# Key rotation permuted by VectorE's writes, norm squares in bf16 with twice the places, mask loads moved past the first gates, scheduler rules and estimates revised

## The chip, the cores and the metric

One Trainium2 chip, all 8 cores running one program, one batch element each. The metric is the device time of the slowest core, in microseconds (us). A program on all cores has a second, slower state in some of its executions, in which the cores of one die have a lower granted TensorE clock; only executions of the fast state are compared here. Because the slowest of eight cores is a noisy pick, I also give the mean of the eight cores.

## The reference, cut to what matters

Two decoder layers on x of 8 x 4096 x 1024. Each layer is a SwiGLU block, a mixer and a second SwiGLU block, each behind an RMS norm with shift, scale and gate from a conditioning vector.

```python
y = modulate(rmsnorm(h, norm_g[l, 1]), sh2, sc2)
proj = y @ w_in[l]                                # u, v of the gating unit; q, k, v of the attention
out_a = spatial_gating(u_a, v_a, ...)             # v is normalised, multiplied by a causal 128 x 128 matrix, gated by u
q_b = apply_rope(q_b, cos, sin); k_b = apply_rope(k_b, cos, sin)
out_b = dilated_mixture(q_b, k_b, v_b)            # windows (128,1), (512,4), (2048,16): keys gathered by stride
h = h + g2 * (concat(out_a, out_b) @ w_out[l])
```

## The kernel before

The kernel is written as operations with an engine (or a choice of engines) and an **estimate in nanoseconds**. A list scheduler in the kernel plays these estimates through when the program is built, and so fixes the order of instructions on every engine and, where there is a choice, the engine. Each engine then runs its list strictly in order.

The rotation of q and k: four products on VectorE, two sums on GpSimd. Keys leave GpSimd permuted, so that the strided attention reads them in order. The value normalisation may go to ScalarE or GpSimd:

```python
for (x, z) in ((0, 0), (1, 1), (0, 1), (1, 0)):
    G.op([dve(lambda e, ...: e.tensor_tensor(out=ap, in0=bank(bks[x]), in1=cs[:, z, :], op=ALU.mult), 610)], ..., name="rope")
for h_ in range(2):
    fr = [[128, 4], [8, 16], [1, 8]]
    to = fr if qk == 0 else [[128, 4], [1, 16], [16, 8]]
    f = lambda e, ...: e.tensor_tensor(out=cust(o, 0, to), in0=cust(a0[0], 0, fr), in1=cust(a1[0], 0, fr), op=...)
    G.op([pool(f, 1800)], reads=[a0[1], a1[1]], writes=[bo], name="ropeadd")
    G.dma("sp", ..., 131072, reads=[bo], accw=[bd[t]], name="qkst")
# vnorm(s), for each of 4 heads
G.op([act(lambda e, ...: e.activation(out=o, in_=i_, func=AF.Identity, scale=sc, bias=bi), 390), pool(f, 500)], ..., name="vnorm")
```

The norm: ScalarE squares eight pieces of a tile into a ring of places, GpSimd adds them up, one small matmul sums over partitions, VectorE multiplies the tile by the result ("nu").

```python
sqR = Ring([NM, NM + 2048], [128, T], F32, "sq")          # also used for "nu"
```

One rule of the scheduler: an instruction whose inputs the estimate has ready later than its turn is put off only if it lies well ahead of the main chain of matmuls.

```python
if not t.dma and t.L > hp + 5000.0 and t.mready > t.ready:
    m = t.mready + min(6000.0, 0.5 * (t.L - hp - 5000.0))
```

The softmax here doesn't subtract the row's maximum and nothing guards it: scores larger than these inputs give would overflow.

Of the kernel before, what the change touches and what calls it, by code (L numbers as in the profile page):

```python
# [7 lines left out]
F32 = mybir.dt.float32  # L8
# [4 lines left out]
D = 1024  # L13
# [55 lines left out]
class Graph:  # L69
# [30 lines left out]
    def _new(self, name, pos):  # L100
        t = Task()
        t.id = len(self.tasks)
        t.name = name
        t.pos = pos
        t.cur = self.M if pos is None else pos
        t.L = None
        t.wl = None
        t.main = False
        t.due = None
        t.part = None  # L110
        t.soft = ()
        t.banks, t.new = [], []
        t.nbytes, t.dma = 0, False
        t.eng = None
        t.tok = None
        t.succ = []
        self.tasks.append(t)
        return t
# [95 lines left out]
    def schedule(self, bw=300.0, dlat=2300.0, dmargin=3000.0, cmargin=250.0, backlog=9000.0):  # L214
# [65 lines left out]
        def pick(e, now):  # L280
# [3 lines left out]
            if e == "pe":  # L284
# [4 lines left out]
                for t in av:  # L289
                    if best is not None and (t.mready <= now, -t.pos) <= bk:  # L290
                        continue
                    if t.new:
                        i, f = find_places(t.new, now)
                        if i is None:
                            nxt = min(nxt, f)
                            continue
                        n = sum(b.n for b in t.new)
                        if (t.pos > hp + 4000.0 or n > 1) and t.name != "up" and sum(x <= now for x in pfree["ps"]) < self.RESERVE + n:
                            nxt = min(nxt, max(now + 50.0, sorted(pfree["ps"])[self.RESERVE + n - 1]))
                            continue  # L300
                    best, bk = t, (t.mready <= now, -t.pos)
# [5 lines left out]
            for t in av:  # L307
# [11 lines left out]
                if not t.dma and t.L > hp + 5000.0 and t.mready > t.ready:  # L319
                    m = t.mready + min(6000.0, 0.5 * (t.L - hp - 5000.0))  # L320
                    if m > now:
# [254 lines left out]
def build_nc():  # L576
# [37 lines left out]
    with ExitStack() as st:  # L614
# [115 lines left out]
        sqR = Ring([NM, NM + 2048], [128, T], F32, "sq")  # L730
# [24 lines left out]
        def cond(chunks, pos, slots, cslot, due=None):  # L755
# [7 lines left out]
                  due=None if due is None else due - 90000.0)  # L763
# [4 lines left out]
            ring = Ring(slots, [128, D], F32, "ada")  # L768
# [33 lines left out]
        def load_gu(l, w, j, pos):  # L802
# [3 lines left out]
            if (l, w) == (0, 0) and (l, w, j) not in kept:  # L806
                G.dma("pool", lambda e: e.dma_start(out=ap, in_=wgu_d[l, w, j]), 1048576, writes=[b], name="guf", pos=pos,
                      due={0: -41000.0, 1: -31000.0, 2: -25000.0, 3: -24000.0, 4: -1000.0}.get(j), extra=[first[(8, 11, 13, 15)[min(j, 3)]]] if j < 6 else ())
# [41 lines left out]
        def main(ins, banks, name, soft=()):  # L850
            p = G.M
            t = G.chain(ins, banks, name, soft=soft)
            marks.append((p, t))
# [53 lines left out]
        def norm_y(ht, slot, l, i, pos, alts=0, apart=False):  # L907
# [6 lines left out]
            for kc in range(KC):  # L914
                hk, bh = ht.ap[:, kc, :], ht.b[kc]
                u, bu = (sq_more[0] if sq_more else sqR).take() if apart else (hk, bh)
# [28 lines left out]
        class FFN:  # L945
# [5 lines left out]
            def gates(self, tiles, slots, reset=True):  # L951
# [5 lines left out]
                for j in range(FC):  # L957
                    gu, bgu = load_gu(self.l, self.w, j, G.M)
                    for t in tiles:
                        y, by = Y[t % 4]  # L960
                        banks = [Bank(), Bank()]
                        for half in range(2):
                            bk = banks[half]
                            main([(lambda e, kc=kc, half=half, bk=bk, y=y, gu=gu: e.matmul(  # L964
                                bank(bk), lhsT=gu[:, half, kc, :], rhs=y[:, kc, :], start=(kc == 0), stop=(kc == KC - 1)),
                                [bgu, by[kc]], MM) for kc in range(KC)], [bk], "gate" if half == 0 else "up", self.act[t][1][j].last())
# [51 lines left out]
        class Mixer:  # L1018
# [24 lines left out]
            def open(self, more):  # L1043
# [3 lines left out]
                sq_more[:] = [Ring([NM, NM + 2048] + steps(more[0], 2048, 2), [128, T], F32, "sq")]  # L1047
# [40 lines left out]
            def proj(self, t):  # L1088
# [67 lines left out]
                def qkpart(qk, g):  # L1156
                    bks = [chunk(8 + qk * 4 + g * 2 + h_, False) for h_ in range(2)]
                    tt = []
                    for (x, z) in ((0, 0), (1, 1), (0, 1), (1, 0)):
                        ap, b = self.tr.take()  # L1160
                        tt.append((ap, b))
                        G.op([dve(lambda e, x=x, z=z, ap=ap: e.tensor_tensor(out=ap, in0=bank(bks[x]), in1=cs[:, z, :],  # L1162
                                                                             op=ALU.mult), 610)],
                             reads=[bks[x], bcs], writes=[b], name="rope")
                    dst, bd = (qS, bQS) if qk == 0 else (kS, bKS)
                    for h_ in range(2):
                        o, bo = self.qk.take()
                        a0, a1 = (tt[0], tt[1]) if h_ == 0 else (tt[2], tt[3])
                        fr = [[128, 4], [8, 16], [1, 8]]
                        to = fr if qk == 0 else [[128, 4], [1, 16], [16, 8]]  # L1170
                        f = lambda e, o=o, a0=a0, a1=a1, h_=h_: e.tensor_tensor(  # L1171
                            out=cust(o, 0, to), in0=cust(a0[0], 0, fr), in1=cust(a1[0], 0, fr),
                            op=ALU.add if h_ else ALU.subtract)
                        G.op([pool(f, 1800)], reads=[a0[1], a1[1]], writes=[bo], name="ropeadd")
                        to_ = bass.AP(dst.tensor, dst.offset + (g * 256 + h_ * 32) * S + t * T, [[64 * S, 4], [S, 32], [1, T]])
                        G.dma("sp", lambda e, o=o, to_=to_: e.dma_start(out=to_, in_=o), 131072, reads=[bo], accw=[bd[t]],
# [44 lines left out]
        class Attn:  # L1221
# [51 lines left out]
            def load_v(self, p, r, pos):  # L1273
# [6 lines left out]
                if r == 1:  # L1280
# [3 lines left out]
                    G.dma("sp", lambda e: e.dma_start(out=v, in_=src), 128 * (16 - n0) * 384, reads=rd, writes=[b],  # L1284
# [3 lines left out]
                for n in range(n0, SB // st_):  # L1288
                    src = bass.AP(vS.tensor, vS.offset + (T0 + n * st_) * VW + p * 192, [[r * VW, 128], [VW, r], [1, 192]])
                    i0 = (n - n0) * r  # L1290
                    G.dma("sp", lambda e, src=src, i0=i0: e.dma_start(out=v[:, i0:i0 + r, :], in_=src), 128 * r * 384,  # L1291
# [159 lines left out]
        for b_ in range(2):  # L1451
            for pc_ in range(2):
                G.dma("pool", lambda e, b_=b_, pc_=pc_: e.dma_start(
                    out=mk_sb[:, :, b_ * 256 + pc_ * 128:b_ * 256 + pc_ * 128 + 128],
                    in_=mk_d[:, :, pc_ * 256 + b_ * 128:pc_ * 256 + b_ * 128 + 128]), 196608, accw=[bC["mk"]], name="mk", pos=100000.0)
# [3 lines left out]
        for l in range(DEPTH):  # L1459
# [3 lines left out]
            def nrm(t, i, pos, src_=None, off=HB):  # L1463
                s, b = (src, bsrc) if src_ is None else src_
                first = l == 0 and i == 0
                norm_y(norm_load(t, s, b, pos, off, {0: -60000.0, 1: -26000.0}.get(t) if first else None), t % 4, l, i, pos, (1 if t == 0 else 3) if l == 0 and i == 0 and t < 4 else 0)
# [9 lines left out]
            if l == 0:  # L1476
                conv(0, 0, [(p1 + 40000.0, pg)], False)
# [207 lines left out]
```

## Time and profile before

| | kernel before |
|---|---|
| time, median of 3 runs | 4878.17 us (4877.49 to 4881.88) |
| mean of the eight cores, profiled run | 4863.5 us |
| TensorE busy, slowest core | 4758.2 of 4881.1 us |
| first gate matmul, median of the cores | 53.2 us |
| four stretches of projection, medians of the cores | 139.7 + 183.6 + 137.7 + 183.6 us |

TensorE is the bound, so a reader looks for the places where it stands still, and for what ended each wait. These groups are the ones that the rotation touches (columns: line, engine, operation, output and input, shapes, count; then busy us and mean ns; then idle time before them and what ended it), kernel before:

```profile
L1162 DVE TENSOR_TENSOR arena<-ps,arena 128x512 f32<-128x512 f32 x256 | 164.3, 681 | 63.1 <-PE ps L1102 35.9 <-POOL arena L1171 24.5 <-POOL arena L895 1.4
L1171 POOL TENSOR_TENSOR arena<-arena 128x512 bf16<-128x512 f32 x128 | 233.6, 1872 | 126.3 <-DVE arena L1162 121.7 <-DVE arena L1127 4.0 <-DVE arena L1133 0.2
L1143 POOL TENSOR_SCALAR arena<-arena 128x128 bf16<-128x128 f32 x26 | 18.9, 734 | 0.0
```

L1162 are the products, L1171 the sums (straight for q, permuted for k, mixed in one mean), L1143 the value normalisations that fell to GpSimd.

### The profile page before, as it was taken

Reading aid. Unit: us, or ns where it says so; the run is one execution under the profiler, and the core shown is the slowest. Engines: PE = TensorE matmul, PEld = TensorE weight load, DVE = VectorE, ACT = ScalarE, POOL = GpSimd, SP = SyncE. Lnnn points to the kernel's source line nnn. Section 1 sums busy time; section 2 is a strip of 40 time slices with the busy share of each in tenths; the row PEclk is TensorE's granted clock in tenths of the full one; section 3 lists DMA queues with packets and bytes.
Section 4 is the critical chain, followed back from the end, with each engine's and each line's share of the span. In section 5 each row is a group of like instructions: output and inputs, shape, how many; then the busy total and the mean of one; then the engine's idle time right before and its main releaser. Section 6 shows DMA issues by size and latency. Waiting matters only on the chain.

```text
span 4881.1 us, 74319 instructions; the slowest of 8 cores (4846.7 to 4881.1 us)
## 1 busy us (share of the span) xinstructions
PE 4758.2 (97%) x25855; PEld 2250.7 (46%) x25855; DVE 2428.5 (50%) x4088; ACT 2044.3 (42%) x3040; POOL 1053.6 (22%) x922
## 2 busy tenths in 40 slices
PE   5999999999999999999999999999999999999998
PEld 2444445444445454444444444454444455544443
DVE  5552556473655373665334326554536654535533
ACT  4111566462755352521311127655537443525311
POOL 0001551112631111310200026412136200123101
PEclk9999999999999999999999999999999999999999
DMA  8977686687575777665721375767665645473414
GB/s 233 207 165 184 171 226 163 177 233 200 160 223 145 192 219 210 208 195 141 237 84 38 92 220 148 218 153 180 154 179 175 195 135 151 117 246 129 143 42 157
DMA packets 376095, 835.31 MB, mean 171 GB/s; under 512 B 151440, under 2 KB 184592, under 8 KB 369296
## 3 DMA queue, kind: packets, MB, share of 16 engines
q1 hardware_dynamic: 356944, 742.08, 49.4%
q0 software_dynamic: 18784, 88.49, 11.7%
q8 instruction: 212, 3.47, 0.3%
q14 instruction: 155, 1.27, 0.1%
HBM read 741.72 MB, written 234.88 MB: 200 GB/s over the span
## 4 chain that ended last, share of the span: by engine, by line
PE 87%; DMA 4%; SPq 3%; ACT 2%; DVE 2%; issue 1%; POOL 1%; DVEq 0%; ACTq 0%; POOLq 0%
PE ps L964 46%; PE ps L992 24%; PE ps L1102 8%; PE ps L1426 4%; PE ps L1368 3%; PE ps L1334 2%; DMA arena<-xP 1%; DMA arena<-hS 1%; SPq L1291 1%; DMA arena<-qS 1%; DVE arena L917 1%; SPq L776 0%; SPq L1435 0%; POOL arena L895 0%; SPq L1188 0%
## 5 line engine op out<-in xcount | busy, mean ns | idle before, releaser
L964 PE MATMUL ps<-arena 128*128 128x512 bf16 x11264 | 2505.1, 380 | 44.0 <-DVE arena L921 32.4
L964 PEld LDWEIGHTS ps<-arena 128*128 128x128 bf16 x11264 | 1082.0, 98 | 1318.1 <-issue 70.4
L992 PE MATMUL ps<-arena 128*128 128x512 bf16 x5632 | 1230.5, 379 | 1.0 <-DVE arena L996 1.0
L970 ACT ACTIVATE arena<-ps 128x512 f32<-128x512 f32 x704 | 418.1, 597 | 1242.4 <-PE ps L964 1233.6
L972 DVE SCALAR_TENSOR_TENSOR arena<-arena,ps 128x512 f32<-128x512 f32 x704 | 480.7, 685 | 770.4 <-ACT arena L970 769.7
L992 PEld LDWEIGHTS ps<-arena 128*128 128x128 bf16 x5632 | 547.5, 98 | 655.7 <-issue 5.2
L895 POOL TENSOR_TENSOR arena<-arena 128x512 f32<-128x512 f32 (+1 forms) x351 | 455.8, 1299 | 1122.2 <-ACT arena L888 1029.8
L996 DVE SCALAR_TENSOR_TENSOR arena<-ps,arena 128x512 f32<-128x512 f32 x256 | 192.1, 751 | 902.4 <-PE ps L992 893.5
L977 DVE TENSOR_TENSOR arena<-ps,arena 128x512 bf16<-128x512 f32 x704 | 484.3, 690 | 202.6 <-PE ps L964 182.4
L1102 PE MATMUL ps<-arena 128*128 128x512 bf16 x2560 | 570.3, 381 | 10.0 <-ACT arena L1153 4.0
L888 ACT ACTIVATE arena<-arena 128x512 f32<-128x512 f32 x424 | 257.2, 626 | 757.2 <-DVE arena L996 387.8
L1352 ACT ACTIVATE arena<-ps 128x1024 bf16<-128x1024 f32 (+1 forms) x384 | 344.6, 949 | 294.5 <-PE ps L1334 291.9
L1102 PEld LDWEIGHTS ps<-arena 128*128 128x128 bf16 x2560 | 249.3, 98 | 309.2 <-issue 20.9
L1355 DVE TENSOR_TENSOR arena<-arena 128x1024 bf16<-128x1024 bf16 (+1 forms) x384 | 258.6, 679 | 141.1 <-ACT arena L1352 139.3
L1404 POOL TENSOR_TENSOR arena<-arena 64x512 bf16<-64x512 f32 x128 | 165.5, 1293 | 592.3 <-ACT arena L1399 545.2
L923 ACT ACTIVATE arena<-arena 128x512 bf16<-128x512 f32 x371 | 276.4, 805 | 36.8 <-DVE arena L917 36.3
L917 DVE TENSOR_TENSOR arena<-arena 128x512 f32<-128x512 f32 x384 | 261.5, 731 | 37.8 <-ACT arena L903 35.0
L1171 POOL TENSOR_TENSOR arena<-arena 128x512 bf16<-128x512 f32 x128 | 233.6, 1872 | 126.3 <-DVE arena L1162 121.7
L1426 PE MATMUL ps<-arena 128*128 128x512 bf16 x1024 | 227.1, 381 | 2.6 <-DMA arena<-mS 2.6
L1384 DVE TENSOR_TENSOR arena<-ps,arena 128x512 f32<-128x512 f32 x256 | 175.5, 685 | 69.7 <-PE ps L1368 63.6
L1368 PEld LDWEIGHTS ps<-arena 128*128 128x128 bf16 x2736 | 174.8, 98 | 76.0 <-issue 16.6
L1368 PE MATMUL ps<-arena 128*128 128x128 bf16 x2736 | 198.7, 220 | 9.1 <-DVE arena L1355 8.5
(66 smaller groups left out, 2075.2 us busy)
## 6 DMA issues: line engine op xcount, KB each, us to landing
arena<-wguS SPq DMA_DIRECT2D x242, 512.0 KB, 7.8
arena<-hS SPq DMA_DIRECT2D x180, 512.0 KB, 8.6
arena<-wdS SPq DMA_DIRECT2D x128, 704.0 KB, 6.0
arena<-ada_w SPq DMA_DIRECT2D x144, 512.0 KB, 18.0
hS<-arena SPq DMA_DIRECT2D x224, 256.0 KB, 5.2
arena<-hS SPq DMA_DIRECT2D x136, 256.0 KB, 6.8
wguS<-wgu POOLq DMA_DIRECT2D x66, 512.0 KB, 7.7
hS<-arena SPq DMA_DIRECT2D x64, 512.0 KB, 6.9
```

Source lines behind the costliest of these rows:

```text
L895: f = lambda e, a=a, sq=sq, out=out: e.tensor_tensor(out=out, in0=a, in1=sq, op=ALU.add)
L917: f = lambda e, hk=hk, u=u: e.tensor_tensor(out=u, in0=hk, in1=rs, op=ALU.mult)
L923: ga = act(lambda e, hk=hk, A=A, sh=sh, o=o: e.activation(out=o, in_=hk, func=AF.Identity, scale=A, bias=sh), 725)
L964: main([(lambda e, kc=kc, half=half, bk=bk, y=y, gu=gu: e.matmul(bank(bk), lhsT=gu[:, half, kc, :], rhs=y[:, kc, :], start=(kc == 0), stop ...
L970: G.op([act(lambda e, sg=sg, gb=gb: e.activation(out=smv[sg.i], in_=bank(gb), func=AF.Tanh, scale=0.5), 490, "tanh")], reads=[gb], writes= ...
L972: G.op([dve(lambda e, sg=sg, gb=gb: e.scalar_tensor_tensor(out=smv[sg.i], in0=smv[sg.i], scalar=1.0, in1=bank(gb), op0=ALU.add, op1=ALU.mu ...
L977: G.op([dve(lambda e, sg=sg, ub=ub, o=o: e.tensor_tensor(out=o, in0=bank(ub), in1=smv[sg.i], op=ALU.mult), 610)], reads=[ub, sg], writes=[ ...
L992: main([(lambda e, j=j: e.matmul(bank(bk), lhsT=wd[:, j, :], rhs=a[:, j, :], start=(j == 0), stop=(j == FC - 1)), [bwd, ba[j]], MM) for j ...
L1102: ins.append((lambda e, lhs=lhs, rhs=rhs, kc=kc: e.matmul(bank(bk), lhsT=lhs, rhs=rhs, start=(kc == 0), stop=(kc == KC - 1)), rd + [by[kc] ...
L1352: return e.activation(out=cut(pT, 0), in_=cut(ps[:, :, :], sb.i * 512), func=AF.Exp, scale=0.125)
L1368: return e.matmul(o, lhsT=v[:, vi, h * 64:h * 64 + 128], rhs=pT[:, h, b, pc, :], start=(pc == 0 or not prev), stop=(pc == 1))
L1426: main([(lambda e, kc=kc, m=m, bk=bk: e.matmul(bank(bk), lhsT=w[:, m, kc, :], rhs=mx[:, kc, :], start=(kc == 0), stop=(kc == KC - 1)), [bw ...
```

## The change

The intent: GpSimd's permuted writes are slow, so let VectorE write the key products permuted and GpSimd add contiguously; give the squares slack; get the mask loads out of the way of the first weights; let the scheduler be more careful. The core of it:

```diff
-sqR = Ring([NM, NM + 2048], [128, T], F32, "sq")
+sqR = Ring(steps(NM, 1024, 4), [128, T], BF16, "sq")
+nuR = Ring(steps(NM, 2048, 2), [128, T], F32, "nu")        # 8 and 4 places in the projection
...
+    def f(e, ...):
+        if qk == 0:
+            return e.tensor_tensor(out=ap, in0=bank(bks[x]), in1=cs[:, z, :], op=ALU.mult)
+        fr = [[128, 4], [8, 16], [1, 8]]
+        return e.tensor_tensor(out=cust(ap, 0, [[128, 4], [1, 16], [16, 8]]), in0=cust(bank(bks[x]), 0, fr),
+                               in1=cust(cs, z * T, fr), op=ALU.mult)
+    G.op([dve(f, 610)], ..., name="rope")                   # the estimate stays
...
-            out=cust(o, 0, to), in0=cust(a0[0], 0, fr), in1=cust(a1[0], 0, fr), ...
-        G.op([pool(f, 1800)], ..., name="ropeadd")
+            out=o, in0=a0[0], in1=a1[0], ...
+        G.op([pool(f, 1350)], ..., name="ropeadd")
...                                      # scheduler: deferral also near the main chain; "up" follows its "gate"
-    if not t.dma and t.L > hp + 5000.0 and t.mready > t.ready:
-        m = t.mready + min(6000.0, 0.5 * (t.L - hp - 5000.0))
+    if not t.dma and t.mready > t.ready:
+        m = t.mready + max(0.0, min(6000.0, 0.5 * (t.L - hp - 5000.0)))
...                                      # cost guesses of two kinds of DMA
-    G.dma("sp", ..., 131072, ..., name="qkst")
+    G.dma("sp", ..., 180000, ..., name="qkst")
-    G.dma("sp", ..., 128 * (16 - n0) * 384, ..., name="av")
+    G.dma("sp", ..., 128 * (16 - n0) * 700, ..., name="av")
...                                      # start: masks after the ninth matmul chain, weight loads gated later, x earlier
-    extra=[first[(8, 11, 13, 15)[min(j, 3)]]] if j < 6 else ()
+    extra=[first[(10, 12, 14, 15, 19)[min(j, 4)]]] if j < 6 else ()
```

## The prediction

> **What bounds the kernel now.** I read the page first, then the cores, the waits of TensorE, the chain of waits in order of time, and stretches of 20 to 200 us.
>
> The page's first part and the cores:
>
> ```profile
> PE 4758.2 (97%) x25855; PEld 2250.7 (46%) x25855; DVE 2428.5 (50%) x4088; ACT 2044.3 (42%) x3040; POOL 1053.6 (22%) x922
> core 0: 4881.1 us, clock 0.994
> core 6: 4846.7 us, clock 0.996
> ```
>
> TensorE is busy for 4758.2 of 4881.1 us: only 122.9 us of the slowest core are not matmul time. If the matmuls stay (the built orders of both kernels have 25,857 each), the time cannot fall below about 4758 us plus a start and an end, so a gain of 2% (98 us) is all but excluded. The cores run one program, yet differ by 34 us: part of what the slowest loses is late data, not arithmetic. By stretches of 200 us, core 0's idle TensorE time is 59.2 us in the first stretch, 5.0 and 8.5 in 400 to 800, 4.1 in 1000 to 1200, 7.0 and 2.9 in 1400 to 1800, 2.6 in 2000 to 2200, 3.7 and 8.7 in 2800 to 3200, about 4.6 elsewhere, and 16.6 at the end.
>
> Who ends these gaps (the waits of TensorE on core 0):
>
> ```profile
> PE ps L964 <- DVE arena L921: 32.4, 1, 32.4
> PE ps L899 <- DVE arena L895: 24.1, 2, 21.8
> PE ps L1368 <- DVE arena L1355: 8.5, 8, 4.1
> PE ps L964 <- DMA arena<-wguS: 4.9, 2, 4.5
> PE ps L899 <- POOL arena L895: 3.9, 2, 2.4
> PE ps L1102 <- ACT arena L1153: 4.0, 1, 4.0
> ```
>
> The first two are the start: nothing but one small matmul runs until the first gate at 54.7 us. The others are short stalls. The chain of waits shows what lies behind them:
>
> ```profile
> 30.96 30.44 DMA arena<-xP
> 65.48 3.57 PE ps L964 x8
> ...
> 605.49 17.47 DMA arena<-xP
> ...
> 630.88 2.36 POOL arena L1171
> ...
> 637.63 0.38 PE ps L899
> ```
>
> The start hangs on the input of tile 1, not only on the 16 modulation rows: the transfer of x lands 30 us after issue. At 605 to 638 us the chain runs from a late tile through GpSimd's key rotation (L1171) to the norm-sum matmul (L899). After a stall the matmuls are slow for a while: 8 of them take 3.57 us at 65.48, against about 0.215 us each in the undisturbed stretch 200 to 400 (929 in 200 us).
>
> **The Trainium skill.** "TensorE: Matmul & The Clock Gate", Part 1, says that the array's clock drops after an idle window of about 3.4 us and returns after a busy one. The trace agrees: 3.57 us for 8 matmuls, and 7.8 us for 24 after the 4.0 us stall at 674 us, where 24 x 0.215 = 5.2 us is normal, a second loss of 2.6 us. "DMA: Bandwidth & Descriptors", Queues, rings and completion order, says that each engine takes packets in turn from the queues that have work; so GpSimd's queue takes from SyncE's even where SyncE's transfers were issued first. The trace agrees: in 0 to 60 us the two shared the engines, which were full,
>
> ```profile
> q1 hardware_dynamic: 4115, 13.03, 72.0%
> q0 software_dynamic: 1394, 2.38, 25.1%
> ```
>
> "Advanced Engine Details and Errata", Memory Cachelines, says that an access to another 16-byte line each time costs extra in SBUF. GpSimd shows it: the 64 query rotations (contiguous) take 1.27 us, the key rotations, which write bf16 with a step of 32 bytes, about 2.4. Whether VectorE pays it too for f32 written with a step of 64 bytes no instruction of this trace shows.
>
> **The change part by part.**
>
> Key rotation. 128 products on VectorE (half of L1162's 256, 0.681 us each) now write permuted; the 64 key sums on GpSimd become contiguous. L1171 is 233.6 us for 128; 64 at 1.27 are 81, so the key half is 152.6 / 64 = 2.38 us each. Gain on GpSimd: 64 x (2.38 - 1.27) = 71 us, or 4.4 us in each of 16 tiles. The built order gives part back: GpSimd's normalisations of v go from 26 to 58, 32 x 0.73 = 23 us. On VectorE I expect 0.68 to at most 1.3 us per permuted product, so 0 to 80 us, 0 to 5 us per tile. In the projection stretches (540 to 680 us) VectorE is about 60 to 80% busy, so this hides. None of it is on TensorE; it counts only through stalls.
>
> Norm squares. Their ring goes from 2 to 4 places (8 in the projection), and scaled rows get their own. ScalarE's 0.626 us and GpSimd's 1.30 us stay (the sums stay f32). What is gained is slack: ScalarE can square ahead of GpSimd's additions. At the end of the kernel nothing moves: the built order still has both last norm-sums behind the last down matmul, so the 17 us tail stays.
>
> Start. Two of the four mask loads (in front at 1.6 us) and two more at 49 us go behind the ninth chain of matmuls; gate-weight loads 1 to 3 wait for the 13th, 15th and 16th modulation row as issued instead of the 11th, 13th and 15th, and loads 4 and 5 for tile 1's input. By windows, SyncE's queue used 39.7 us of full-engine time up to 52 us, GpSimd's 10.3 (masks 2.5, the first weight load 3.2, the rest 4.6). I expect some 5 us of the latter left, so the last row lands 5 us sooner and the first gate starts near 50 instead of 54.7 us. But the new order puts tile 1's norm sum after 16 gate matmuls, not 32. Tile 1's last squares came at 70 us, with 19.7 us of GpSimd's queue ahead; now only four weight loads are ahead, 4 x 3.2 = 12.7 us, so near 63 us. The norm sum then ends near 65 instead of 71.9 us, with 16 matmuls (3.5 us) more left to do. Net gain: 7.0 - 3.5 = 3.5 us, rather than 4.7.
>
> Scheduler. A row load for attention counts almost double (700 for 384 bytes), operations with uncertain inputs are put off more cautiously, and an up chain follows its gate. The built SyncE order changes mostly at the turns into attention: three gate-weight loads instead of one now stand between the two kinds of v loads where TensorE stalled 4.5 us on wguS at 1448 us.
>
> The sum for core 0: start -3.5. In the projection stages of both layers stalls of about 9.8 + 2.1 and 3.7 + 8.7 us, with some 12 us of slow clock behind them (clock 0.97 over two stretches of 200 us: 0.03 x 400); I estimate that 40% of these 36 us go: -14. The attention and turn stalls (4.1 + 7.0 + 2.9 + 2.6 + about 3, and 5 of clock) are about 25; a fourth goes: -6. Together -24 us: 4878 - 24 = 4854; I take 4857, since the slowest of eight cores keeps the worst stalls. The two fractions are my choice; the profile gives only the pool from which they draw.
>
> **The rivals.**
>
> A. VectorE becomes the stage's bound. If the permuted writes cost 1.3 us or more, four key products take over 5 us, about as long as the 24 matmuls beside them (5.2 us); the ring of four products and the banks then back up. For it: TensorE already waits on banks freed by VectorE and ScalarE there. Against it: two of four rotations per tile are queries, and GpSimd loses 4.4 us per tile. With 2 us lost in each of the 8 tiles least filled with other work: +16 on the sum, about 4870.
>
> B. Late inputs stay. In 655 to 673 us ScalarE waits 3.7 and 4.3 us for x before squares, and its later GELU then frees a bank late (the 4.0 us stall). More places for squares do not bring x earlier, and the new order puts norm sums 32 to 56 matmuls sooner, in trust of a faster GpSimd. If x is as late as before, TensorE stands before the norm sum: about 3 us in some four places and as much of slow clock, +24 on the sum: about 4878.
>
> C. The start is worth more, if x of tile 1 and the rows both land 7 us sooner and tile 0's four weights suffice: -7, and all stalls of projection halved: near 4840.
>
> **Range and chances.** The sum gives -24; rival A about -8, B about 0, C about -38. I widen both ends by the spread of the cores: 4830 to 4884. Faster by over 2% would need under 4780, less than matmuls plus start and tail (4758 + 50 + 17), so 1%; slower by over 2% would need 98 us of new stalls, conceivable only if VectorE's permuted writes cost several times more: 1%.
>
> **What would show it.** L1171 near 1.27 us in all 128 and the sum near 163 us; the permuted products in a row of their own, at 0.7 us (else A); the first gate near 50 us and tile 1's norm sum ending near 65; squares unchanged near 0.63 us; the waits of L1102 and L899 after 500 us lower in both layers, with the clock of 600 to 800 and 3000 to 3200 above 0.97; the tail still 17 us. I am wrong if norm sums wait longer than before (B), if ropes hold the banks (A), or if the slow cores 0, 2, 4 and 7 do not come nearer to 1, 3, 5 and 6.

## The result, and the profile after

The fast runs of the changed kernel took 4889.81, 4890.12 and 4893.37 us. Ratio to the kernel before **1.0025**, 95% interval [1.0005, 1.0045]. Ratios here are the mean time of one kernel's fast runs over that of the other's of the same rounds, so not quite the ratio of the medians. It is the class that was predicted (within 2%), but 12 us slower where 21 us faster was expected, and above the range of 4830 to 4884.

The page's first part, two of the cores, and the rotation's groups of the kernel after, in the columns shown before:

```profile
PE 4755.4 (97%) x25855; PEld 2250.5 (46%) x25855; DVE 2466.9 (50%) x4087; ACT 2026.2 (41%) x3009; POOL 987.9 (20%) x954
core 1: 4888.1 us, clock 0.995
core 3: 4860.4 us, clock 0.997
L1169 DVE TENSOR_TENSOR arena<-ps,arena 128x512 f32<-128x512 f32 x128 | 81.8, 680 | 20.6 <-PE ps L1106 14.1 <-POOL arena L1178 5.5 <-DMA arena<-rope 0.9
L1171 DVE TENSOR_TENSOR arena<-ps,arena 128x512 f32<-128x512 f32 x128 | 119.5, 1025 | 20.2 <-PE ps L1106 13.8 <-POOL arena L1178 6.1
L1178 POOL TENSOR_TENSOR arena<-arena 128x512 bf16<-128x512 f32 x128 | 168.4, 1324 | 165.8 <-DVE arena L1169 115.1 <-DVE arena L1171 45.9 <-DVE arena L1131 4.2
L1147 POOL TENSOR_SCALAR arena<-arena 128x128 bf16<-128x128 f32 x58 | 40.5, 710 | 2.6 <-DVE arena L1137 2.6
```

All busy times did what was intended: GpSimd's sums 233.6 to 168.4 us, VectorE's permuted products 1.03 us each in place of 0.68, TensorE the same. The start did too; the waits of TensorE in the first 80 us of core 0 (columns: engine, tile and line, releaser; us in total, times, longest):

```profile
PE ps L967 <- DVE arena L924: 26.9, 1, 26.9
PE ps L902 <- DVE arena L898: 19.7, 1, 19.7
PE ps L886 <- ACT arena L884: 9.8, 3, 4.7
```

The first two lines answer to the 32.4 and 21.8 us of the kernel before: the first gate comes 6 us sooner. The third is new: tile 1's squares. They end 7 us sooner than before (at 62.3 in place of 69.4 us, medians of the cores), but the order now puts them behind 16 gate matmuls instead of 32, so TensorE runs out of work before they come.

To see where the 6 us and more went, I cut the span at stages that both kernels pass (the last matmul of each group of gates, downs and projections), on every core, and compared the medians over the cores. On two of the eight cores of every profile some 2% of the matmul records are missing; there a stage ends at the gap between two groups, not at a count. (The expectations below quote an earlier cut without this care; it was up to 1 us off in the projections of these two kernels and about 3 us in layer 0's attention.) Differences to before: start -6.2; gates and downs of tiles 0 to 3 of layer 0 +2.2; **the four stretches of projection +6.2, +3.5, +4.6 and +2.5, together +16.8**; the gates and downs of tiles 4 to 7 -5.6; **the second half of the attention** (the second SwiGLU's gates and downs 0, 1 and gates 2, 3, beside which it runs) **-0.1 in layer 0 and +5.2 in layer 1**; the tail 17.7 us in both. All differences together are 11.9; the mean of the cores rose by 12.0. Layer 0's first projection took 136 to 137 us on four cores of the kernel before and 143 to 147 on the other four, so its median lies between two groups; layer 1's is the cleaner measure: 136 to 139 us on seven of the cores before, 140 to 146 on all eight after.

The waits of TensorE in layer 1's first projection, core 2, kernel before (2941 to 3078 us) and then kernel after (2939 to 3082 us):

```profile
PE ps L1102 <- ACT arena L1118: 2.1, 1, 2.1
PE ps L1193 <- ACT arena L923: 1.8, 1, 1.8
PE ps L1102 <- ACT arena L1145: 0.7, 1, 0.7
```

```profile
PE ps L1199 <- POOL arena L1147: 3.9, 3, 1.6
PE ps L1106 <- ACT arena L1122: 2.7, 1, 2.7
PE ps L1106 <- ACT arena L1149: 0.7, 1, 0.7
```

The new wait is that of the gating matmuls (L1199) for value normalisations on GpSimd (L1147). (L1118, after L1122, is the values' GELU, L1145 or L1149 the normalisation on ScalarE, L923 or L926 the scaling of the normed tile, L1157 the GELU of u.) Averaged over the cores, the waits of this stretch are 8.3 us after against 5.2 before; in layer 0's first projection 10.3 against 6.7. Why such a normalisation is late is seen on the engines' timelines of the same core (start, duration, then as above; x5 is five in a row):

```profile
2959.82 6.15 DVE L920 TENSOR_TENSOR arena<-arena 128x512 f32<-128x512 f32 x8
2961.61 5.53 POOL L1147 TENSOR_SCALAR arena<-arena 128x128 bf16<-128x128 f32 x5
2965.58 0.22 PE L1199 MATMUL ps<-arena 128*128 128x128 bf16 x1 [1.37 <-POOL arena L1147]
2967.40 0.22 PE L1199 MATMUL ps<-arena 128*128 128x128 bf16 x1 [1.60 <-POOL arena L1147]
```

Five normalisations take 5.53 us while VectorE multiplies two operands from SBUF (L920); of the 58 on a core, 14 lie beside L920 and take 0.9 to 1.9 us, and the other 44, beside key products (PSUM and one SBUF operand) or nothing, take 0.44. The Trainium skill, "SBUF — State Buffer", Who interferes with whom, states this: a VectorE instruction with two SBUF inputs contends with a GpSimd instruction that reads SBUF; their shared ports are an exclusive lock, and the order of issue decides which of the two blocks. It made a tempting theory, which the experiments below did not bear out as the cause of the loss.

### The profile page after: what moved, and what is told of

Its sections match the earlier page's. It is cut to its first block, busy times and chain, and to the rows that moved or that the text cites. A ratio compares the mean times of both kernels' runs of the same rounds, so it can differ in the third digit from the quotient of the medians.

```text
span 4888.1 us, 74266 instructions; the slowest of 8 cores (4860.4 to 4888.1 us)
## 1 busy us (share of the span) xinstructions
PE 4755.4 (97%) x25855; PEld 2250.5 (46%) x25855; DVE 2466.9 (50%) x4087; ACT 2026.2 (41%) x3009; POOL 987.9 (20%) x954
## 4 chain that ended last, share of the span: by engine, by line
PE 86%; DMA 5%; ACT 3%; DVE 2%; issue 2%; SPq 1%; POOL 1%; DVEq 0%; ACTq 0%; POOLq 0%
PE ps L967 47%; PE ps L995 24%; PE ps L1106 5%; PE ps L1432 4%; PE ps L1374 3%; PE ps L1340 2%; DMA arena<-xP 1%; DMA hS<-arena 1%; DMA arena<-hS 1%; DVE arena L1171 1%; ACT arena L1149 1%; DMA kS<-arena 0%; POOL arena L1147 0%; SPq L778 0%; POOL arena L1178 0%
## 5 line engine op out<-in xcount | busy, mean ns | idle before, releaser
L898 POOL TENSOR_TENSOR arena<-arena 128x512 f32<-128x512 f32 (+2 forms) x351 | 414.3, 1180 | 1160.4 <-ACT arena L891 1056.9
L891 ACT ACTIVATE arena<-arena 128x512 bf16<-128x512 f32 x424 | 250.5, 625 | 723.9 <-DVE arena L999 384.6
L1361 DVE TENSOR_TENSOR arena<-arena 128x1024 bf16<-128x1024 bf16 (+1 forms) x384 | 261.5, 687 | 148.7 <-ACT arena L1358 146.4
L926 ACT ACTIVATE arena<-arena 128x512 bf16<-128x512 f32 x372 | 279.5, 806 | 52.3 <-DVE arena L920 51.9
L920 DVE TENSOR_TENSOR arena<-arena 128x512 f32<-128x512 f32 x384 | 271.9, 757 | 35.7 <-ACT arena L906 30.4
L1410 POOL TENSOR_TENSOR arena<-arena 64x512 bf16<-64x512 f32 x128 | 168.4, 1316 | 598.5 <-ACT arena L1405 557.9
L1374 PEld LDWEIGHTS ps<-arena 128*128 128x128 bf16 x2736 | 175.4, 98 | 73.8 <-issue 12.9
L1374 PE MATMUL ps<-arena 128*128 128x128 bf16 x2736 | 199.2, 219 | 7.4 <-DVE arena L1361 6.8
L1178 POOL TENSOR_TENSOR arena<-arena 128x512 bf16<-128x512 f32 x128 | 168.4, 1324 | 165.8 <-DVE arena L1169 115.1
```

The lines of the kernel that those rows point to most:

```text
L898: f = lambda e, a=a, sq=sq, out=out: e.tensor_tensor(out=out, in0=a, in1=sq, op=ALU.add)
L920: f = lambda e, hk=hk, u=u: e.tensor_tensor(out=u, in0=hk, in1=rs, op=ALU.mult)
L926: ga = act(lambda e, hk=hk, A=A, sh=sh, o=o: e.activation(out=o, in_=hk, func=AF.Identity, scale=A, bias=sh), 725)
L1374: return e.matmul(o, lhsT=v[:, vi, h * 64:h * 64 + 128], rhs=pT[:, h, b, pc, :], start=(pc == 0 or not prev), stop=(pc == 1))
```

## The experiments

Theory 1: the dearer permuted writes lose. Theory 2: the order that the scheduler builds loses, through its rules, its guesses, or the estimate 1350. Theory 3: the normalisations on GpSimd lose. All results below are of fast runs (three to five in each row, from five rounds), beside the kernel before on the same chip. "Slowest" and "mean" are differences in us to the before of the same rounds (slowest core, mean of cores; means over the fast runs). "Proj." is the sum over the four projection stretches, "att." the second half of the attention in both layers, each against before, medians over the cores of the profiled run; one profile each, so differences of 2 us or less in them mean little. In one run each of x3 and x8, two of x9 and three of x1, cores of one die show a slightly lower clock (0.98 to 0.99), too little to be counted as slow; this lengthens the slowest core above all. (The mean of the changed kernel, 4877.0, is held against the 4863.5 of the profiled run of before.)

| run | edit | slowest | mean | ratio [95%] | start | proj. | att. |
|---|---|---|---|---|---|---|---|
| after | the whole change | +12.2 | +13.5 | 1.0025 [1.0005, 1.0045] | -6.2 | +16.8 | +5.0 |
| x1 | start alone | +14.6 | +0.8 | 1.0029 [0.9995, 1.0064] | -7.0 | +5.3 | -1.5 |
| x2 | rotation, estimate 1800 | -3.3 | -4.0 | 0.9992 [0.9976, 1.0008] | -0.2 | -2.8 | -2.6 |
| x3 | after, straight products | +6.5 | +7.5 | 1.0013 [0.9993, 1.0033] | -7.1 | +12.1 | +3.0 |
| x4 | after, GpSimd permutes | +19.8 | +21.3 | 1.0040 [1.0024, 1.0056] | -6.8 | +28.0 | +6.8 |
| x5 | rotation, estimate 1350 | +13.9 | +19.0 | 1.0028 [1.0014, 1.0042] | -0.5 | +11.2 | +3.3 |
| x6 | squares alone | -1.0 | +5.0 | 0.9998 [0.9985, 1.0011] | -1.1 | +1.6 | +1.1 |
| x7 | rules and guesses alone | +3.1 | +3.3 | 1.0004 [0.9985, 1.0023] | -0.6 | +5.8 | +3.1 |
| x8 | after, old rules and guesses | +25.9 | +24.2 | 1.0053 [1.0020, 1.0086] | -7.3 | +16.6 | +5.6 |
| x9 | after, estimate 1800 | +16.1 | +6.6 | 1.0034 [0.9976, 1.0091] | -7.3 | +0.1 | +3.0 |
| x10 | after, no normalisation on GpSimd | +24.4 | +30.9 | 1.0051 [1.0035, 1.0067] | -6.4 | +25.1 | +9.1 |
| x11 | x5, no normalisation on GpSimd | +26.3 | +30.4 | 1.0057 [1.0039, 1.0075] | +0.7 | +18.8 | +4.7 |
| x12 | before, estimate 1350 | +27.4 | +32.8 | 1.0057 [1.0039, 1.0075] | +0.1 | +19.3 | +5.6 |
| x13 | after, fills for normalisations | +7.9 | +9.4 | 1.0016 [1.0000, 1.0032] | -6.8 | +15.8 | +5.0 |
| x14 | after, 1800, old guesses | -2.7 | -1.9 | 0.9992 [0.9971, 1.0014] | -7.1 | +0.2 | 0.0 |
| x15 | after, key products at 1040 | **-10.5** | **-7.4** | **0.9979 [0.9963, 0.9994]** | -7.3 | -0.2 | +1.9 |
| x16 | x14, normalisations to VectorE | +10.1 | +12.1 | 1.0021 [1.0005, 1.0036] | -6.7 | +9.5 | +2.9 |
| x17 | x5, key products at 1040 | +3.1 | +4.9 | 1.0005 [0.9991, 1.0019] | +0.7 | +2.7 | +1.8 |
| x18 | x15, old guesses | -10.3 | -1.9 | 0.9979 [0.9966, 0.9991] | -6.4 | -0.7 | +1.1 |

### x1 to x4: the parts, and the writes against the order

**x1**, the start alone (masks, gates of the weight loads, x earlier; no other hunk).

> The kernel before with the start's part alone (mask loads behind the ninth chain, later gates for the first weight loads, order of the modulation rows). In the changed kernel the first gate came about 6 us earlier and 1 to 2 us were given back in the first gates stage. If the start's gain does not depend on the other parts: first gate near 47 us, 4 to 5 us faster than before in the mean of the cores, all later stages within 1 us, about 4874 us. If the start only moves work into the crowded stage that follows: 0, about 4878 us.

The first gate came 7.0 us sooner, yet the mean of the cores was the same as before; the gain went in the following stages (gates and downs of tiles 0 to 3 +3.4, projections +5.3). Its slowest core varied from 4876 to 4915 us, so the slowest core alone would mislead.

**x2**, the rotation's instructions in the exact order of before. Only the estimate keeps that order:

```diff
-        G.op([pool(f, 1350)], reads=[a0[1], a1[1]], ...)
+        G.op([pool(f, 1800)], reads=[a0[1], a1[1]], ...)
```

> The kernel before, in exactly its order of instructions, with only the key rotation changed (VectorE writes permuted, GpSimd adds contiguous). Theory 1, the permuted writes cost more than they save (1.03 instead of 0.68 us, 44 us in all, in stages where VectorE feeds the banks): the projection stages 4 to 6 us longer each in the first half and 2 to 3 in the second, about 4890 us. Theory 2, the operations are a gain and the new order loses it: 2 to 6 us faster than before, about 4874 us, key sums at 1.27 us.

The same permuted products, at the same price, in the run x2:

```profile
L1167 DVE TENSOR_TENSOR arena<-ps,arena 128x512 f32<-128x512 f32 x128 | 121.2, 1030 | 17.3 <-PE ps L1102 15.5 <-POOL arena L1174 1.7
```

The kernel was 4.0 us faster in the mean of cores, and all projections together 2.8 us shorter than before. So the rotation does not lose by what its instructions cost.

**x3**, the changed kernel's order with straight key products (wrong result, relative error 0.152), and **x4**, the same order with GpSimd permuting as before:

```diff
-                            if qk == 0:
+                            if qk < 2:            # x3; x4 in addition writes the sums of k permuted on GpSimd
```

> The changed kernel in exactly its order, but key products written straight on VectorE (keys stay unpermuted: wrong result on purpose). Theory 1: products 0.68 us, the projection stages 10 to 14 us shorter in all than in the changed kernel, about 4877 us. Theory 2: VectorE is 44 us less busy, but the stages stay within 3 us of the changed kernel, about 4888 us.

> The changed kernel in exactly its order, with the key rotation as before (straight products on VectorE, permuted sums on GpSimd at 2.4 us; correct result). Theory 1: close to the time before or below it, 4872 to 4880 us, because VectorE's 44 us go and the start's gain stays. Theory 2: the order counts on a GpSimd that is now 71 us busier: longer than the changed kernel by 5 to 15 us, 4895 to 4905 us.

In the changed order, straight products take the projections' loss from +16.8 to +12.1: about a quarter of it comes with the permuted writes, three quarters stay without them. x4's sums, the line to hold against L1178 above:

```profile
L1178 POOL TENSOR_TENSOR arena<-arena 128x512 bf16<-128x512 f32 x128 | 233.6, 1891 | 147.8 <-DVE arena L1169 145.3 <-DVE arena L1131 1.3 <-DMA qS<-arena 0.6
```

With them the projections lose 28.0 us in that order, against 16.8: moving the permutation to VectorE is right, in either order. Theory 1 falls as the main cause.

### x5 to x8: which part of the new order

**x5** is x2 with the change's estimate of 1350, so it differs from x2 by one number. **x6** is the squares alone, **x7** the scheduler's rules and DMA guesses alone, **x8** the change without those.

> Kernel before with the key rotation of the change and its new estimate for the GpSimd sums (1350 in place of 1800); nothing else. By the built order the value normalisations on GpSimd rise from 26 to 54 of 128, which is the only thing that distinguishes it from the run with the old order (4875.6 us mean, 4 us under the kernel before in the mean of cores). Theory 'estimate': the lower estimate makes GpSimd look free and the scheduler gives it normalisations in the projection stages, for whose release TensorE then waits: the first projection stage (139.7 us before, 141.9 with the old order) goes to 144 to 147, the span to about 4885. Theory 'rules': the loss of the changed order comes from the scheduler's new rules, not from this estimate: span 4873 to 4880, first projection stage at most 143. Neither expects anything in the second half of the attention (its three stages together within 1 us of before).

> Kernel before with the squares in bf16, four places and their own ring for the products, alone. Theory 'squares gain': GpSimd's sums of norms are 0.12 us cheaper each and the squares run earlier, so the stalls of the start and of the reloads fall slightly: span 4873 to 4878. Theory 'reordering': every shift of the greedy schedule deals the waits anew, with no systematic gain: span 4874 to 4888, with the squares of the next norm run ahead of the values' products and stores, so that the stage after the first projection starts with the late key load. If the second half of the attention loses 3 us a layer here, the ring of squares is its cause.

> Kernel before with only the scheduler's new rules and estimates (the deferral of instructions that would make an engine wait, the pairing of gate and up, the higher cost guesses of two kinds of DMA); no arithmetic, tile or engine form changes. Theory 'rules': these alone lose what the changed kernel loses in the second half of the attention (3 us a layer there) and part of the projection: span 4884 to 4892, the mean of cores 4869 to 4876. Theory 'rotation': the rules are neutral, span 4874 to 4882, and no stage moves by more than 2 us.

> The changed kernel with the scheduler's old rules and old DMA guesses: rotation (with the new estimate), squares and start only. Theory 'rules': it keeps the start's 6 us, loses nothing in the second half of the attention, and lands at 4870 to 4880. Theory 'estimate': the 56 normalisations on GpSimd stay, so the first projection stage stays at 144 or more and the span at 4882 to 4892.

x5 answers: the same instructions, one estimate changed, and the mean of cores goes from -4.0 to +19.0, the projections from -2.8 to +11.2. My stage figure for layer 0's first projection missed (142.0 us, expected 144 to 147), layer 1's (143.1 us, 137.7 before) shows it instead. x6 is neutral on the slowest core, though 5 us worse in the mean of cores. x7 is nearly neutral, and shows where layer 1's second half of the attention loses; I had expected 4884 to 4892 under the theory of rules, and it was 4881.5. x8 is worse than the changed kernel, also without its one run with a disturbed die (+14.6 and +21.9 then): the new rules and guesses do not cause the loss but lessen it.

### x9 to x12: the estimate, and the normalisations on GpSimd

**x9** puts 1800 back in the changed kernel; **x12** puts 1350 into the kernel before, with no other edit. **x10** and **x11** forbid GpSimd the normalisations:

```diff
-                            out=o, in_=i_, func=AF.Identity, scale=sc, bias=bi), 390), pool(f, 500)],
+                            out=o, in_=i_, func=AF.Identity, scale=sc, bias=bi), 390)],
```

> The changed kernel with one number put back: the estimate of GpSimd's sum of rotated products, 1350 to 1800. Arithmetic, tiles and engine forms are those of the changed kernel; the normalisations on GpSimd fall from 58 to 38. Theory 'estimate' (now the leading one: rotation with the old estimate was 4 us faster in the mean of cores, with the new one 19 us slower): this recovers most of the loss: slowest core 4872 to 4882 (the changed kernel: 4890), mean of cores 4858 to 4866 (changed: 4877), and the first projection stage of layer 0 at 143 us or less (changed: 146.2), of layer 1 at 140 or less (142.7). Theory 'any reordering loses': this is just one more order of the same greedy schedule and lands anywhere from 4876 to 4895, with the projection stages no better than the changed kernel's.

> The changed kernel with its estimates, but the values' normalisations allowed on ScalarE alone (0 of 128 on GpSimd in place of 58). Theory 'normalisations': it is these that the low estimate lets onto GpSimd, two tenths of a microsecond longer there and queued ahead of the sums, so this recovers as much as the old estimate: slowest core 4874 to 4882, layer 1's first projection at 140 or less. Theory 'sums early': the loss is how early the low estimate makes the scheduler place the sums and what waits behind them, the normalisations are a bystander: 4884 to 4894, the projection stages within 1.5 us of the changed kernel's. ScalarE becomes busier in the projection, so a loss above 4894 would say that GpSimd's help was needed.

> The kernel before with the key rotation of the change and its new estimate (that run was 4892 us, 4878.5 in the mean of cores), and the values' normalisations on ScalarE alone (0 in place of 54). Theory 'normalisations': back to 4874 to 4880, mean of cores 4857 to 4863. Theory 'sums early': 4885 to 4894, as with the 54.

> The kernel before, its arithmetic and engine forms untouched (GpSimd still writes the keys permuted, 2.4 us in place of 1.3), with the new estimate of 1350 alone. Theory 'estimate': the order built from that number is what loses, whoever permutes: 4888 to 4900, at least as slow as the run with the rotation and the new estimate (4892), because GpSimd's sums are longer still. Theory 'permuted writes on VectorE': with straight products the order costs nothing: 4875 to 4882.

x9's projections are back at the length of before (+0.1 in place of +16.8). Its slowest core is inconclusive: two runs took 4872.3 and 4873.7 us, two others 4901 and 4929 with one die at a clock of 0.98 to 0.99. x12 loses 19.3 us in the projections with not one instruction form changed: **the estimate alone makes a loss of this size**. (At 4905 us it is a little slower than the 4888 to 4900 expected.) x10 and x11 refute theory 3 in its plain form: with no normalisation on GpSimd the projections are worse still; ScalarE is then the one waited for.

### x13 to x16: the port, the guesses, and true numbers

**x13** keeps the changed kernel's order on every engine and replaces the normalisations on GpSimd by fills, which read nothing (wrong, relative error 0.143). **x14** is x9 with the old DMA guesses. **x15** changes one number of the changed kernel to what the trace shows. **x16** is x14 with the normalisations on ScalarE or VectorE, at an estimate of 250 for VectorE.

```diff
-    f = lambda e, ...: e.tensor_scalar(out=o, in0=i_, scalar1=sc, scalar2=bi, op0=ALU.mult, op1=ALU.add)
+    f = lambda e, o=o: e.memset(o, 0.0)                                  # x13
...
-    G.op([dve(f, 610)], reads=[bks[x], bcs], writes=[b], name="rope")
+    G.op([dve(f, 610 if qk == 0 else 1040)], reads=[bks[x], bcs], writes=[b], name="rope")      # x15
...
-    ... bias=bi), 390), pool(f, 500)],
+    ... bias=bi), 390), dve(f, 250)],                                    # x16
```

> The changed kernel in its exact order on every engine; only the 58 value normalisations that GpSimd does are replaced by a fill of their place with zeros, which reads no SBUF (wrong result on purpose). Theory 'port': in the changed kernel's trace a normalisation on GpSimd takes 0.44 us beside VectorE's rotated products but 1.3 to 1.9 us beside its norm products, which read two operands from SBUF; TensorE's wait for it (3.2 us in layer 0's first projection, 3.9 in layer 1's, 1.2 and 0 before) goes, every fill takes about the same time whatever VectorE does, and the mean of cores falls from 4877 to 4864 to 4870. Theory 'places': the early places of the sums lose, the normalisations are a bystander: the waits move to other producers, mean of cores 4873 to 4879.

> The changed kernel with two of its estimates put back: the GpSimd sums' 1350 to 1800, and the cost guesses of the value loads and of the stores of q and k to those of before. Rotation, squares, start and the two scheduler rules stay. Theory 'guess': the loss in the second half of the attention (its first three stages together +3 us in layer 0, +5 in layer 1, as in the run that had the rules alone) comes from the guesses, since the built order of that part follows them and not the rules; it goes, and with the old estimate the mean of cores is 4852 to 4858, slowest core 4864 to 4872: faster than both kernels. Theory 'rules': the loss stays, mean of cores 4860 to 4864, slowest 4872 to 4876.

> The changed kernel with the estimate of VectorE's key products put to their measured time, 610 to 1040; GpSimd's sums keep 1350 (measured 1.27 to 1.32). Theory 'true numbers': the lower estimate lost only because its counterpart on VectorE stayed 40% too low; with both right the projection stages come back (layer 0's first at 142 or less, layer 1's at 139 or less), mean of cores 4858 to 4867. Theory 'port': 72 normalisations are on GpSimd now, and the estimates still know nothing of what stretches them: projection stages as the changed kernel's or worse, mean of cores 4873 to 4885.

> As the run without the guesses (old estimate 1800, old DMA guesses), but the value normalisations are allowed on ScalarE or VectorE in place of ScalarE or GpSimd. Theory 'port': with none on GpSimd nothing waits for that port on the path[...]: projection stages 1 to 3 us below that run's. Theory 'load': VectorE already carries the dearer products (28 us more in all) and gets later with the rotated products that TensorE's banks wait for: projection stages 2 to 6 us above that run's.

In x13 the five that took 5.53 us take less than a microsecond, on the same core in the same place (GpSimd's timeline):

```profile
2945.08 0.78 POOL L1147 MEMSET arena<- 128x128 bf16 x5
```

So the port's block is real, and fills don't suffer it. But the waits of TensorE in layer 1's first projection, core 2 (2923 to 3063 us), only changed their names:

```profile
PE ps L1106 <- ACT arena L1122: 2.8, 1, 2.8
PE ps L1106 <- DVE arena L1204: 1.6, 2, 1.4
PE ps L1106 <- DVE arena L1171: 1.6, 2, 1.4
```

Averaged over the cores they are 7.5 us against 8.3 (10.1 against 10.3 in layer 0); the projections stay at +15.8. The next producers stand right behind the one that was named. The mean of cores, 4872.2, is a little better than theory 'places' had it (4873 to 4879) and short of theory 'port' (4864 to 4870): some 4 us of 13, and not in the projections.

x15, one number put right, takes the projections to -0.2. The same stretch on core 2 (2911 to 3048 us):

```profile
PE ps L1106 <- ACT arena L1157: 1.8, 1, 1.8
PE ps L1199 <- ACT arena L926: 1.2, 1, 1.2
```

Averaged, 5.0 us here and 5.8 in layer 0. It does this with 72 normalisations on GpSimd, more than the 58 of the changed kernel, and 12 of them are still stretched beside L920 (14 there): in this order TensorE no longer waits for them, which speaks against theory 3 once more. x15 is the fastest kernel, correct, and faster than both: 4868.7 us, mean of four runs, against 4879.2 for the before of its rounds. x16 goes the way of the load theory (projections 9.3 us above x14's), but it doesn't prove it: a normalisation on VectorE took 0.32 to 0.36 us, and nine of the 58 on core 1 took 1.1 to 1.3, against the 250 of the estimate, so its order too was built from a wrong number.

x14 settles where layer 1's second half of the attention loses. The middle window of it in layer 1 (downs 0 and 1; columns: the window, its length, then busy us and count of TensorE, weight load, VectorE, ScalarE, GpSimd, then the granted clock, DMA share, GB/s), first the kernel before on core 0, then after on core 0, then x14 on core 1:

```profile
3997.00:4085.00 88.00, 88.00 (x576) 44.33 (x574) 29.45 (x43) 24.12 (x31) 10.13 (x8) 1.00 0.66 195
```

```profile
3977.00:4065.00 88.00, 85.15 (x581) 43.71 (x580) 31.25 (x45) 27.75 (x36) 10.21 (x8) 0.98 0.61 183
```

```profile
3970.00:4058.00 88.00, 88.00 (x576) 44.26 (x574) 29.33 (x42) 24.14 (x31) 10.13 (x8) 1.00 0.65 197
```

The changed order has a hole of nearly 3 us there, and the clock falls from 1.00 to 0.98. The wait that makes it (after, core 0, 3780 to 4259 us):

```profile
PE ps L1374 <- DVE arena L1361: 3.0, 2, 2.7
```

A product of the attention with its values (L1374) has been put where VectorE's masking (L1361) has not yet ended. The stall costs twice, as TensorE's timeline of that core shows with the same 22 matmuls before and behind it:

```profile
4045.65 4.92 PE L995 MATMUL ps<-arena 128*128 128x512 bf16 x22
...
4054.93 0.61 PE L1374 MATMUL ps<-arena 128*128 128x128 bf16 x8 [2.67 <-DVE arena L1361]
...
4056.44 6.08 PE L995 MATMUL ps<-arena 128*128 128x512 bf16 x22
```

With the old guesses the hole is gone, and x14 keeps the new rules, so it comes from the guesses: the waits of L1374 for VectorE in this stage are 2.4 to 3.0 us on every core after, 0.3 on every core of x14 and of before. In layer 0 they are 3.4 to 4.7 us after, but there the stage loses nothing: its gates 0 and 1 gain 4.6 us, what follows loses 4.4. The mean of cores, expected at 4852 to 4858, was 4860.9: held against x9, which differs by the guesses alone, gates and downs of tiles 0 to 3 lose 2.8 us, those of tiles 4 to 7 2.1 and 1.3 us. What one order gains in a place, it gives back in another.

### x17 and x18: does it carry over?

**x17** is the rotation alone with 1350 and 1040; **x18** is x15 with the old DMA guesses.

> The kernel before with the key rotation of the change, GpSimd's sums at 1350 and VectorE's key products at 1040 in place of 610; nothing else. The same with 610 was 4892 us, 4878.5 in the mean of cores; the rotation in the order of before was 4875.6 and 4859. Theory 'true numbers': 4868 to 4878, mean of cores 4853 to 4863, layer 1's first projection at 139 or less (143.3 with 610), though 74 normalisations are on GpSimd (54 with 610). Theory 'a lucky order': the gain of the changed kernel with that number doesn't carry over: 4880 to 4895.

> The changed kernel with VectorE's key products at 1040, and the DMA guesses of the value loads and of the stores of q and k put back to those of before. With the guesses of the change this was 4868.7 and 4855.4 in the mean of cores. Theory 'guess': the second half of the attention regains about 1.4 us in layer 0 and 4.2 in layer 1 and nothing else moves: mean of cores 4849 to 4852, slowest core 4861 to 4866. Theory 'given back': what a later order of that part gains is lost in other stages, as without the guesses before (mean of cores 4860.9 against 4861.6): mean of cores 4853 to 4860.

x17 landed between its theories: 14 of x5's 19 us in the mean of cores come back, but not the gain; layer 1's first projection stays at 140.5 us (139 or less expected). x18 is given back, as its rival said, and more: the attention regains only 0.8 us, the gates and downs of tiles 4 to 7 lose 8.1, the slowest core is no better than x15's, and the mean of cores (4863.0) lies above the 4853 to 4860 expected.

## Why the prediction was wrong, point by point

- **What bounds the kernel, the floor, and the class: right.** TensorE's busy time moved by 2.8 us; nothing was to be had or lost but stalls.
- **The instructions' costs: right.** GpSimd's sums at 1.32 us (expected 1.27) and 168 us (163); the permuted products 1.03 us, in the middle of 0.68 to 1.3; squares unchanged at 0.625; the tail unchanged at 17.7. One miss: GpSimd's additions of squares were to stay at 1.30 us, and took 1.16 to 1.19.
- **The start: right in its place.** Tile 1's squares were expected near 63 us and ended at 62.3. Expected net -3.5; start plus the gates and downs of tiles 0 to 3 gave -6.2 + 2.2 = -4.0. Alone (x1) it is given back in later stages. In x15 it is kept.
- **The step that failed: "40% of these 36 us go: -14".** It measured +16.8. I read the stalls of the projection as slack that cheaper sums would fill, and took the built order as neutral. I had the evidence in hand that it was not: normalisations on GpSimd from 26 to 58. I charged them as 23 us of busy time on an idle engine, and took VectorE's added busy time (44 us as measured, 128 x 0.345) as hidden likewise. Busy time was the wrong coin: what counts on in-order engines is where the list puts an instruction against its real duration. In the projections the changed rotation loses nothing in orders built with 1800 (x2, x9, x14), and 1350 beside 610 builds orders that lose 11 to 19 us even with the rest of the kernel as before (x5, x12).
- **"A fourth goes: -6" for the attention and the turns: it did not come.** The attention's second half lost 5.2 us in layer 1, by a wait that the DMA guesses ordered in (x14); the gates and downs of tiles 4 to 7 gave 5.6 back.
- **The signs that it named.** The clock of 600 to 800 and 3000 to 3200 us was to rise above 0.97 and stayed there (0.97 on core 1). The slow cores 0, 2, 4 and 7 did come level with 1, 3, 5 and 6, but because these lost 26 us while the former gained 2 (in these two executions; which cores are slow differs from one to the next).
- **Its sums.** Rival C's -38 does not follow from its own terms: -7 at the start, 18 for half of the projection's stalls and 6 elsewhere make -31. The range's ends were widened by 10 and 6 us, not by the 34 us between the cores that the text names.
- **Rival A** (VectorE becomes the bound) had the right place and about a quarter of the size (x3 against after: 4.7 of 16.8). **Rival B** (late inputs, norm sums too early) named a neighbour: in the changed kernel TensorE waited at most 0.1 us for norm sums in these stretches, and x15, which wins, places them about as early.
- **What is shown, and what is open.** Shown: the estimate 1350 beside an untouched 610 is the cause of the projections' loss (x5 against x2, x12 against before, x9 and x15 against after). The parts do not add: the start alone (x1) and the rules and guesses alone (x7) each show 5 to 6 us there, but x9, which has both, nothing. Not shown: that true numbers as such make a good order. x3 made both numbers nearly true in the changed order (0.68 us for 610, 1.31 for 1350) and still lost 12.1 us, and x17 recovered only three quarters. My reading, argued only, is that 1800 had been a cushion for other estimates that are off: a normalisation on GpSimd takes 0.44 to 1.9 us for an estimate of 500. Which of these makes one order good was not settled. Each set of estimates gives one order, so that x15 is the best of these by luck is not excluded either.

## What to carry to other kernels

Where a scheduler orders in-order engines from estimates, an estimate is part of the program: change an instruction's form, and every number it touches must be measured again, on the engine that got dearer as well as the one that got cheaper. To price such a change before a run, compare the built orders and test the new instructions in the old order; a releaser named by a wait is only the last of several, and removing it may move the wait to the next. Judge 8 cores by the mean of the cores and by stages, since the two differed by up to 14 us in one run (x1).

## What the Trainium skill lacked or had wrong

- "Advanced Engine Details and Errata", Memory Cachelines, says that a new 16-byte line for each access costs, but gives no size; none for writes was found on another page. Here VectorE, writing f32 with a step of 64 bytes, took 1.03 us in place of 0.68 for 128x512 elements, and GpSimd, writing bf16 with a step of 32 bytes, about 2.4 in place of 1.27.
- "SBUF — State Buffer", Who interferes with whom, is borne out: 128x128 on GpSimd took 0.44 us beside VectorE instructions with one SBUF input, up to 1.9 beside those with two, and fills about 0.20 with no difference. What it lacks is the remark that freeing the blocked instruction may win nothing: here fills in place of 58, 14 of them stretched, moved the projections by 1.0 us.
- "TensorE: Matmul & The Clock Gate", Part 1, gives an idle window of about 3.4 us for the clock to drop. Here a stall of 2.67 us was enough: 22 matmuls behind it took 6.08 us, 4.92 before it, and their starts lay 0.427 us apart in place of 0.216 until 4058.9 us. Not every stall of this length does it: counting, in all kept traces, the stalls that stand 8 us or more apart from others (cores with complete records, after the first 200 us), none of 1091 of 0.5 to 1.5 us was followed by such steps, 71 of 285 of 2.0 to 2.6 us, 83 of 126 of 2.6 to 3.4 us, and all 124 of over 5 us.
